# Weight pages moved to 96 bytes past a multiple of 128, and every product's passes as 256-column matmuls

## The chip, the cores and the metric

The kernel runs on one core of one Trainium2 chip. The metric is the device time of one execution in microseconds; the kernel before takes 2318.54 us (median of three runs, 2314.81 to 2322.06).

## The reference, cut to what matters

One layer of an encoder on 512 frames of 2048 features, all in float32: an input projection, banded attention and gated linear attention, an output projection, a gated MLP with a short convolution, a gate from a per-layer embedding, and norms between them.

```python
proj = h @ w_in                                   # then attention and GLA
x = x + concat([y_a, y_g]) @ w_out
u = causal_depthwise_conv(h @ w_ffn_up, w_ffn_conv, b_ffn_conv)
u_gate, u_val = split(u, 2)
x = x + (gelu(u_gate) * u_val) @ w_ffn_down
x = x + sigmoid(rms_norm(x) @ w_ple_gate) * (p @ w_ple_proj)
return rms_norm(x)
```

Nearly all the work is in the matrix products with `w_in`, `w_out`, `w_ffn_up`, `w_ffn_down` and `w_ple_gate`.

## The kernel before, in words

**Three passes.** A float32 product is made of three matmul passes on the format float32r. Each weight page is split into a high part (`wh`, made by ScalarE with a Copy) and a low part (`wl`, made by VectorE as raw minus high), and the operand in the same way. The passes are high weights by high operand, high weights by low operand, low weights by high operand. In each matmul the weights are the stationary operand (loaded by a weight load of 128 columns) and the operand x is the moving one.

**Units and products.** From the attention on, work goes in units. A unit is two blocks of 128 output rows by the two 256-column halves of the frames, computed with seven products in place of eight (P1 to P7, from sums of weight blocks L11, L12, L21, L22 and sums of operand halves R11, R21, R22, N1, N2, T3, T4). One product is kb blocks of 128 by three passes: kb is 8, or 7 in two of the three parts of the down projection. The stages are `in` (12 units, beside the attention), `wo` (8), `up` (44), `dn0` to `dn2` (8 each, kb 8, 7, 7) and `pg` (8). `collect` (L515 to L540) adds a product's PSUM bank into the output page `u`: the first product of a quarter is copied by ScalarE, the others added by VectorE, 128x256 at a time.

**Joined products.** In the middle units of the stages `wo`, `up`, `dn` and `pg` (all but the first two and last two: 4, 40, 4 in each of the three, and 4, so 60 units), products P2, P3 and P4 (`JOINED`, L34) are issued otherwise: the first two passes share the weights, so one matmul of 512 columns reads the high and the low half of x (two runs of 256 that lie 4096 bytes apart) and writes both halves of the bank; the third pass adds into the first half (L495 to L505). `collect` then needs a second VectorE addition of 128x256 for the second half (L536, L537).

**Places in SBUF.** Where a tile begins in its partition follows from the order and sizes of the pools. The pool `pages` holds the weight pages and the pages for x-independent data (`r0`.., `h0`.., `l0`.., `u0`, `u1`, `c0`); behind it lies `h` (the input operand's 16 tiles, moving or stationary in the first 317 us), later replaced by `xb` (operand tiles N1, T3, R22, T4), which begins with a small tile `pad`. From the right end, behind a tile `shim`, lie first the tiles of the gated linear attention, and later `xa` (operand tiles R11, R21, N2). Then come `att` (Q, K and so on of the attention) and `late` (more pages for raw weights and outputs). In this program the begins are, as the remainder by 128 bytes:

| tiles | before | after |
|---|---|---|
| `pages`: weight pages, high and low parts | 0 | 96 |
| `h`: the input operand's tiles | 0 | 96 |
| `xa`, `xb`: the operand tiles of all units | 32 | 32 |
| `att` (Q, K), `late` | 32 | 32 |

All blocks inside these tiles are multiples of 512 bytes, so the remainder holds for every matmul of such a tile. Three products at the very end of `pg` take their weights from operand tiles of `xa` (name `last`), so both operands of these begin at 32.

**What sets the order.** From the attention on, VectorE, ScalarE and TensorE keep the program's order; a table (`agenda`) says after which product each step is issued. A raw page that comes free is refilled at once by SyncE's queue or, where a sum of two blocks is wanted, by GpSimd's accumulating DMA.

Of the kernel before, what the change touches and what calls it, by code (L numbers as in the profile page):

```python
# [8 lines left out]
F32 = mybir.dt.float32  # L9
# [3 lines left out]
ALU = mybir.AluOpType  # L13

P = 128
T = 512
# [14 lines left out]
            "PP": ("L11", None, None)}  # L31
PLAIN = ("P1", "P2", "P6", "P5", "P7", "P3", "P4")
HALVES = ("P1", "P2", "P6", "P7", "P4", "P5", "P3")
JOINED = ("P2", "P3", "P4")  # L34
RINGS = {"wr": ("r0", "r1", "r2"), "wh": ("h0", "h1", "h2"), "wl": ("l0", "l1", "l2")}
FRONT_RINGS = {"u": ("u0", "u1"), "c": ("c0",), "x": ("r6",)}
BACK_RINGS = {"u": ("u2", "u3", "u0", "u1"), "c": ("c1", "c2", "c0"), "x": ("x0", "x1")}
# [5 lines left out]
def encoder_block(ctx: ExitStack, tc: tile.TileContext, A, out):  # L43
    nc = tc.nc
# [4 lines left out]
    pg = ctx.enter_context(tc.tile_pool(name="pages", bufs=1))  # L49
# [7 lines left out]
    class InOrder:  # L57
        def __init__(self, engine):
            self.engine, self.on = engine, False
# [11 lines left out]
    vec, act, ten = InOrder(nc.vector), InOrder(nc.scalar), InOrder(nc.tensor)  # L71
# [26 lines left out]
    def page(ring, name, dt=F32, shape=(P, 1024)):  # L98
        tags = rings[ring]
        i = counts.get(ring, 0)  # L100
        counts[ring] = i + 1
        tag = tags[i % len(tags)]
        return page_pool(tag).tile(list(shape), dt, tag=tag, name=name)
# [99 lines left out]
    def slot(i, name, dt=F32R):  # L203
        return hp.tile([P, 2, T], dt, tag=f"h{i}", name=name)

    pairs = [pg.tile([P, 2, T], F32, tag=t, name=f"pair_{t}") for t in PAIR_TAGS]

    def xslot(i, name):
# [54 lines left out]
    xa, xb = [], []  # L263
# [35 lines left out]
    def xtile(op, g, name, dt=F32R):  # L299
        pool = xa[0] if X_TAGS.index((op, g)) < 6 else xb[0]  # L300
        return pool.tile([P, 2, 1024], dt, tag=f"{op}{g}", name=name)
# [10 lines left out]
    class Stage:  # L312
        def __init__(self, name, units, kb, xd, weights, after, sums, edge, last=PLAIN, begin=None, begin_at=0,
                     chained=False, pace=None, late=(), single=False):
            self.name, self.kb, self.xd, self.weights, self.after = name, kb, xd, weights, after
            self.begin, self.begin_at, self.pace, self.late = begin, begin_at, pace, late
            self.chained, self.tail, self.quarter = chained, [None, None], None
            self.n = (4, kb - 4 - 2 * chained)
            self.x = {}
            n = len(units)  # L320
            self.units = [Unit(self, u, last if i >= n - 2 else PLAIN, edge if i < 2 or i >= n - 2 else sums)
                          for i, u in enumerate(units)]
            for i in range(n):
                self.units[i].pos = i
            if single:
                self.groups = [[u] for u in self.units]
                return
            self.units[0].first = True
            for i in range(2):
                self.units[i].head = i  # L330
                self.units[n - 2 + i].last = i
            self.groups = [self.units[:2]] + [[u] for u in self.units[2:-2]] + [self.units[-2:]]
            for u in self.units[2:-2]:
                u.joined = JOINED

        def load(self, op, g):
            w = self.n[g] * 256
# [21 lines left out]
    class Unit:  # L359
        def __init__(self, stage, u, order, sums):  # L360
            self.stage, self.u, self.order, self.sums = stage, u, order, sums
            self.first, self.head, self.last = False, None, None
            self.w, self.tag = {}, {}
            if sums == "dma":
                self.uses = dict(L11=2, L12=2, S1=2, S2=2, S3=1, L22=1)
                self.made = {"S2", "S4"}
            else:
                self.uses = dict(L11=3, L12=2, S1=2, S2=2, L21=2, L22=2)
                self.made = {"S1", "S2", "S3", "S4"}
            self.parts = dict(C11=2, C12=2, C22=2, C21=1)  # L370
            self.have = set()
            self.left = dict(A=4, B=1, C=2)
            self.o = None
            self.banks = {}
            self.joined = ()

    free = [f"r{i}" for i in (3, 4, 5)]
    wanted = []
# [65 lines left out]
    def prep(i, own=None):  # L444
        prep_low(prep_high(i, own))
# [32 lines left out]
    def bank(name):  # L478
        tag = banks.pop(0)
        return tag, pp_.tile([P, T], F32, tag=tag, name=name)  # L480

    def product(unit, prod, at=None, between=None):
        if prod == "PP":
            return embedding(unit)
        _, op, b = PRODUCTS[prod]
        fresh = b not in unit.banks
        if fresh:
            unit.banks[b] = bank("acc" + b)
        both = unit.banks[b][1]
        t = both[:, 0:256]  # L490
        hi, lo = unit.w[prod]
        st = unit.stage
        kb = st.kb
        kw = {} if fresh else {"skip_group_check": True}
        if prod in unit.joined:  # L495

            for p in range(2):
                for k in range(kb):
                    x = st.x[op, k // 4][:, :, k % 4 * 256:k % 4 * 256 + 256]
                    w = (hi, lo)[p][:, k * P:k * P + P]  # L500
                    if p == 0:
                        ten.matmul(both.rearrange("p (h t) -> p h t", h=2), w, x, start=fresh and k == 0, stop=k == kb - 1, **kw)
                    else:
                        ten.matmul(t, w, x[:, 0], start=False, stop=k == kb - 1, skip_group_check=True)
            return  # L505

        for p in range(3):
            for k in range(kb):
                if p * kb + k == at:
                    between()  # L510
                x = st.x[op, k // 4][:, p % 2, k % 4 * 256:k % 4 * 256 + 256]
                w = (hi, hi, lo)[p][:, k * P:k * P + P]
                ten.matmul(t, w, x, start=fresh and p == k == 0, stop=p == 2 and k == kb - 1, **kw)

    def collect(unit, prod):  # L515

        if prod == "PP":
            return
        b = PRODUCTS[prod][2]
        tag, t = unit.banks[b]  # L520
        t = t[:, 0:256]
        unit.left[b] -= 1
        if unit.left[b] == 0:
            banks.append(tag)
        if unit.o is None:
            unit.o = page("u", "u").rearrange("p (s t) -> p s t", s=2)
        quarter, sign = {"P1": ("C11", 1), "P2": ("C11", 1), "P6": ("C12", 1), "P5": ("C22", -1),
                         "P7": ("C22", -1), "P3": ("C12", 1), "P4": ("C21", -1)}[prod]
        s, h = int(quarter[1]) - 1, int(quarter[2]) - 1
        dst = unit.o[:, s, 256 * h:256 * h + 256]  # L530
        if quarter not in unit.have:
            unit.have.add(quarter)
            act.activation(dst, t, AF.Copy, scale=float(sign))
        else:
            vec.tensor_tensor(dst, dst, t, ALU.add if sign > 0 else ALU.subtract)
        if prod in unit.joined:  # L536
            vec.tensor_tensor(dst, dst, unit.banks[b][1][:, 256:T], ALU.add if sign > 0 else ALU.subtract)  # L537
        unit.parts[quarter] -= 1
        if unit.last is not None and unit.stage.quarter and unit.parts[quarter] == 0:
            unit.stage.quarter(unit, quarter)  # L540
# [328 lines left out]
    for a, b in zip(stages[3:], stages[4:]):  # L869
        i0 = base[a.units[-1]]  # L870
        for n, p in enumerate(PLAIN):
            op = PRODUCTS[p][1]
            for g in range(2):
                start = 2 * n + 2 + g
                if g and b.chained:
                    start = max(start, 5)
# [10 lines left out]
    for n, p in enumerate(PLAIN):  # L887
        op = PRODUCTS[p][1]
# [4 lines left out]
        at, k = ((8, 1), (8, 1), (9, 1), (12, 1), (11, 3), (12, 3), (13, 3))[n]  # L893
# [60 lines left out]
    both = slice(0, 2)  # L954
# [78 lines left out]
            (nc.scalar if c else nc.sync).dma_start(vad[4 * c:4 * c + 4, :, t].rearrange("b p v -> p b v"),  # L1033
                              vstage[c, t].rearrange("p (b v) -> p b v", b=4))

    shim = ctx.enter_context(tc.tile_pool(name="shim", bufs=1, side="right")).tile([P, 240], F32, tag="shim", name="shim")
    nc.gpsimd.memset(shim, 0.0)
    with ExitStack() as mix:
        vp = mix.enter_context(tc.tile_pool(name="v", bufs=1, side="right"))

        with ExitStack() as gctx:
# [8 lines left out]
            for i in range(2):  # L1050
                t = gp.tile([P, T], F32, name=f"attnT{i}")
# [25 lines left out]
            for kt in range(KD):  # L1077
                w = glh[:, kt * 32:kt * 32 + P]
# [117 lines left out]
            st = gla_proj(0)  # L1196
            for hd in range(1, 4):
                nxt = gla_proj(hd)
                gla_core(hd - 1, *st)
                st = nxt  # L1200
# [19 lines left out]
    def operands_left():  # L1220
        hctx.close()
        xb.append(ctx.enter_context(tc.tile_pool(name="xb", bufs=1, reuse_waits="tile")))
        pad = xb[0].tile([P, 8], F32, tag="pad", name="pad")
        nc.gpsimd.memset(pad, 0.0)
        for op in ("N1", "T3", "R22", "T4"):
            for g in range(2):
                front.load(op, g)
        free.extend(("r0", "r1", "r2"))
        issue()
        prep(0)  # L1230
        prep(1)
        for g in range(2):
            front.split("N1", g)
# [16 lines left out]
    for i, (unit, prod) in enumerate(steps[:-4]):  # L1250
        st = unit.stage
# [6 lines left out]
        for k, f in todo:  # L1258
            if k == 1:
                f()  # L1260
        prep_low(coming)
        product(unit, prod)
        for k, f in todo:
            if k > 1:
# [5 lines left out]
        if i - len(steps) in EARLY:  # L1270
            p, op, g = EARLY[i - len(steps)]
            t = xtile(op, g, "last")
# [53 lines left out]
    lo, hi = lo_half, hi_half  # L1326
# [105 lines left out]
```

## Time and profile before

| | |
|---|---|
| median of 3 runs | 2318.54 us (2314.81 to 2322.06) |
| span of the profiled execution, first to last instruction | 2315.0 us |
| mean granted TensorE clock | 0.994 |
| TensorE busy | 2269.1 us, 16564 matmuls |
| VectorE busy | 1957.4 us |
| ScalarE busy | 1295.4 us |
| DMA | 223 GB/s on average |

The profiled execution's own time is its span of 2315.0 us and what lies around it; the median lies 3.5 us above the span. PE is TensorE, PEld its weight loads, DVE VectorE, ACT ScalarE, POOL GpSimd, SP SyncE. A row of the timeline merges matmuls of one kind that follow each other: start, time from the first's start to the last's end, then what it is and how many. Since matmuls overlap, the time from one start to the next (the pitch) is what a matmul costs; it is had from the starts of two rows, divided by the count of the first.

### The profile page before, as it was taken

How to read it: one execution, taken by the hardware profiler on the slowest of the kernel's cores; microseconds unless marked ns; L12 is line 12 of the kernel's file. 1: busy time of each engine (PE TensorE's matmuls, PEld its weight loads, DVE VectorE, ACT ScalarE, POOL GpSimd, SP SyncE). 2: the span in 40 equal slices, each digit the busy share in tenths (PEclk: the TensorE clock that was granted, in tenths of full speed). 3: DMA queues.
4: the chain of work that ended last, by engine and by line, in shares of the span. 5: the costliest groups of instructions: out<-in, count | busy, mean ns of one | idle time of the engine just before them, and what ended most of it. 6: DMA issues, size and time to landing. Idle time of an engine off the chain costs nothing.

```text
span 2315.0 us, 42243 instructions
## 1 busy us (share of the span) xinstructions
PE 2269.1 (98%) x16564; PEld 2122.6 (92%) x16564; DVE 1957.4 (85%) x2753; ACT 1295.4 (56%) x1894; POOL 143.1 (6%) x180
## 2 busy tenths in 40 slices
PE   9999999999999999999999999999999999999996
PEld 8878889999989999999999999999999999999995
DVE  7556358888779888999999999999898797999997
ACT  6344356777555565555555555555564554656655
POOL 0000000000000000000000000000000100000100
PEclk9999999999999999999999999999999999999998
DMA  6522486666978977787877777777866967879994
GB/s 221 195 76 88 168 286 168 177 182 185 314 244 269 309 219 201 214 220 213 219 211 214 206 218 207 218 210 217 261 213 222 316 216 250 282 241 331 273 288 160
DMA packets 195464, 516.48 MB, mean 223 GB/s; under 512 B 20896, under 2 KB 72352, under 8 KB 195264
## 3 DMA queue, kind: packets, MB, share of 16 engines
q1 hardware_dynamic: 165184, 421.49, 51.9%
q0 software_dynamic: 23616, 84.95, 20.8%
q10 hardware_dynamic: 6464, 7.34, 0.9%
q8 instruction: 130, 2.13, 0.4%
q14 instruction: 70, 0.57, 0.1%
HBM read 435.05 MB, written 76.55 MB: 221 GB/s over the span
## 4 chain that ended last, share of the span: by engine, by line
PE 86%; DVE 6%; DMA 4%; ACT 2%; issue 2%; ACTq 0%; DVEq 0%; SPq 0%; POOL 0%; POOLq 0%
PE accA L65 39%; PE accC L65 20%; PE accB L65 10%; PE v L250 2%; PE v L251 2%; PE v L252 2%; DVE wl L65 1%; DMA s<-in_w_blk 1%; DVE u L65 1%; PE pp L65 1%; PE py L65 1%; PE ptr L65 1%; DVE s L65 1%; PE psc L65 1%; PE pk L134 1%
## 5 line engine op out<-in xcount | busy, mean ns | idle before, releaser
L65 DVE TENSOR_TENSOR wl<-s,wh 128x1024 fp32r<-128x1024 f32 (+1 forms) x365 | 437.3, 1199 | 47.3 <-ACT wh L65 46.3
L65 ACT ACTIVATE wh<-l 128x1024 fp32r<-128x1024 f32 (+1 forms) x308 | 318.8, 1037 | 174.9 <-PE accC L65 110.2
L65 ACT ACTIVATE wh<-s 128x1024 fp32r<-128x1024 f32 (+1 forms) x365 | 377.6, 1037 | 48.1 <-DVE s L65 31.8
L65 DVE TENSOR_TENSOR wl<-l,wh 128x1024 fp32r<-128x1024 f32 (+1 forms) x308 | 367.8, 1194 | 39.8 <-ACT wh L65 39.5
L65 ACT ACTIVATE u<-accA 128x256 f32<-128x256 f32 x290 | 109.4, 377 | 339.1 <-PE accA L65 338.9
L65 DVE TENSOR_TENSOR s<-s,l 128x1024 f32<-128x1024 f32 (+1 forms) x192 | 229.5, 1195 | 13.9 <-DMA s<-in_w_blk 12.7
L65 PE MATMUL accA<-up_T,wh 128*128 128x256 f32 (+1 forms) x1088 | 178.6, 313 | 0.2 <-ACT u L65 0.2
L65 PEld LDWEIGHTS accA<-up_T,wh 128*128 128x128 f32 x1088 | 150.1, 188 | 11.4 <-ACT u L65 0.4
L65 DVE SCALAR_TENSOR_TENSOR cv<-u,cw,cv 128x511 f32<-128x511 f32 (+1 forms) x176 | 131.5, 747 | 3.1
L408 POOL DMA_DIRECT2D s<-in_w_up x88 | 75.1, 853 | 788.4 <-DVE u L65 256.7
L65 DVE TENSOR_TENSOR u<-u,accC 128x256 f32<-128x256 f32 x158 | 66.1, 418 | 44.2 <-PE accC L65 41.5
L251 PE MATMUL v<-wv_l,h 128*128 128x512 f32 x256 | 100.5, 392 | 0.0
L250 PE MATMUL v<-wv_h,h 128*128 128x512 f32 x256 | 100.3, 392 | 0.0
L252 PE MATMUL v<-wv_h,h 128*128 128x512 f32 x256 | 99.9, 391 | 0.0
L65 PE MATMUL accA<-up_T,wl 128*128 128x256 f32 x704 | 96.3, 279 | 0.0
L65 ACT ACTIVATE cv<-u,cw 128x512 f32<-128x512 f32 x88 | 67.1, 810 | 51.9 <-DVE u L65 51.9
L65 PEld LDWEIGHTS accA<-up_T,wl 128*128 128x128 f32 x704 | 91.2, 188 | 3.7
L65 PE MATMUL accA<-dn_T,wh 128*128 128x256 f32 (+1 forms) x616 | 90.4, 296 | 2.8 <-ACT wh L65 2.8
L65 PE MATMUL accB<-up_R,wh 128*128 128x512 f32 (+1 forms) x384 | 91.2, 380 | 1.9 <-DVE up_R L65 1.3
L65 PE MATMUL accA<-up_R,wh 128*128 128x256 f32 x704 | 89.7, 279 | 0.0
L65 PE MATMUL accA<-up_N,wh 128*128 128x256 f32 x704 | 89.3, 279 | 0.1
L65 PE MATMUL accC<-up_N,wh 128*128 128x256 f32 x704 | 89.2, 279 | 0.0
(386 smaller groups left out, 5123.2 us busy)
## 6 DMA issues: line engine op xcount, KB each, us to landing
l<-in_w_up SPq DMA_DIRECT2D x132, 512.0 KB, 5.1
s<-in_w_up SPq DMA_DIRECT2D x88, 512.0 KB, 4.6
s<-in_w_up POOLq DMA_DIRECT2D x88, 512.0 KB, 5.7
l<-in_w_dn SPq DMA_DIRECT2D x56, 448.0 KB, 5.0
l<-in_w_blk SPq DMA_DIRECT2D x36, 512.0 KB, 5.1
l<-in_w_out SPq DMA_DIRECT2D x28, 512.0 KB, 5.2
l<-in_w_dn SPq DMA_DIRECT2D x28, 512.0 KB, 5.3
s<-in_w_blk SPq DMA_DIRECT2D x24, 512.0 KB, 4.5
```

Of the source, the lines that this page charges most:

```text
L65: ins = f(*args, **kw)
L134: nc.tensor.matmul(po, whi, act[:, 1, :], start=False, stop=False)
L250: nc.tensor.matmul(ps[t], h1[kt][:, 0, sl], wh, start=kt == 0, stop=False)
L251: nc.tensor.matmul(ps[t], h1[kt][:, 0, sl], wl, start=False, stop=False)
L252: nc.tensor.matmul(ps[t], h1[kt][:, 1, sl], wh, start=False, stop=kt == KD - 1)
L408: nc.gpsimd.dma_start(t, src("L22" if name == "S1" else "L11"), accum_op=ALU.add)
```

## The change

Two things are done. A tile `lead` of 24 floats is put ahead of the pages, so `pages` and `h` begin 96 bytes later; `shim` and `pad` are resized so that `xa`, `xb`, `att` and `late` keep their remainder by 128 (the tiles themselves lie 128 bytes further on). And no product is joined any more: the branch in `product`, the second addition in `collect` and the marks on units go.

```diff
-JOINED = ("P2", "P3", "P4")
...
+    lead = pg.tile([P, 24], F32, tag="lead", name="lead")
+    nc.gpsimd.memset(lead, 0.0)
     pairs = [pg.tile([P, 2, T], F32, tag=t, name=f"pair_{t}") for t in PAIR_TAGS]
...
-            for u in self.units[2:-2]:
-                u.joined = JOINED
...
-        if prod in unit.joined:
-
-            for p in range(2):
-                for k in range(kb):
-                    x = st.x[op, k // 4][:, :, k % 4 * 256:k % 4 * 256 + 256]
-                    w = (hi, lo)[p][:, k * P:k * P + P]
-                    if p == 0:
-                        ten.matmul(both.rearrange("p (h t) -> p h t", h=2), w, x, start=fresh and k == 0, stop=k == kb - 1, **kw)
-                    else:
-                        ten.matmul(t, w, x[:, 0], start=False, stop=k == kb - 1, skip_group_check=True)
-            return
-
...
-        if prod in unit.joined:
-            vec.tensor_tensor(dst, dst, unit.banks[b][1][:, 256:T], ALU.add if sign > 0 else ALU.subtract)
...
-    shim = ctx.enter_context(tc.tile_pool(name="shim", bufs=1, side="right")).tile([P, 240], F32, tag="shim", name="shim")
+    shim = ctx.enter_context(tc.tile_pool(name="shim", bufs=1, side="right")).tile([P, 208], F32, tag="shim", name="shim")
...
-        pad = xb[0].tile([P, 8], F32, tag="pad", name="pad")
+        pad = xb[0].tile([P, 16], F32, tag="pad", name="pad")
```

On TensorE, the product P2 of a middle unit of `up` (bank `accB`, operand tiles `up_R`, weights `wh` and `wl`) stands in the program before as

```order
L65 MATMUL accB<-up_R_8319,wh 128x512 x4
L65 MATMUL accB<-up_R_8362,wh 128x512 x4
L65 MATMUL accB<-up_R_8319,wl 128x256 x4
L65 MATMUL accB<-up_R_8362,wl 128x256 x4
L65 MATMUL accA<-up_N_8396,wh 128x256 x4
```

and in the changed program as

```order
L64 MATMUL accB<-up_R_8405,wh 128x256 x4
L64 MATMUL accB<-up_R_8448,wh 128x256 x4
L64 MATMUL accB<-up_R_8405,wh 128x256 x4
L64 MATMUL accB<-up_R_8448,wh 128x256 x4
L64 MATMUL accB<-up_R_8405,wl 128x256 x4
L64 MATMUL accB<-up_R_8448,wl 128x256 x4
L64 MATMUL accA<-up_N_8482,wh 128x256 x4
```

Eight matmuls of 512 columns have become sixteen of 256; the rest stands where it stood. On VectorE, the rows from the scaling of one unit's output (`u<-u,rb`) to the next unit's product P3 (bank `accC`) are before

```order
L65 TENSOR_TENSOR u<-u,rb 128x1024
L65 TENSOR_TENSOR wl<-s_13111,wh 128x1024
L65 SCALAR_TENSOR_TENSOR cv<-u,cw,cv 128x511
L65 SCALAR_TENSOR_TENSOR cv<-u,cw,cv 128x510
L65 TENSOR_TENSOR wl<-s_12850,wh 128x1024
L65 TENSOR_TENSOR u<-u,accB 128x256 x2
L65 TENSOR_TENSOR s_13111<-s_13111,l_12806 128x1024
...
L65 TENSOR_TENSOR wl<-l_12997,wh 128x1024
L65 TENSOR_TENSOR u<-u,accC 128x256 x2
```

and in the changed program

```order
L64 TENSOR_TENSOR u<-u,rb 128x1024
L64 TENSOR_TENSOR wl<-s_13568,wh 128x1024
L64 SCALAR_TENSOR_TENSOR cv<-u,cw,cv 128x511
L64 SCALAR_TENSOR_TENSOR cv<-u,cw,cv 128x510
L64 TENSOR_TENSOR wl<-s_13279,wh 128x1024
L64 TENSOR_TENSOR u<-u,accB 128x256
L64 TENSOR_TENSOR s_13568<-s_13568,l_13235 128x1024
...
L64 TENSOR_TENSOR wl<-l_13447,wh 128x1024
L64 TENSOR_TENSOR u<-u,accC 128x256
```

The doubled additions have become single ones; nothing else has changed places. ScalarE's order is the same throughout.

More of the change, by code (lines that the diff above doesn't have):

```diff
@@ L374, in __init__ @@
             self.banks = {}
-            self.joined = ()
     free = [f"r{i}" for i in (3, 4, 5)]
@@ L488, in product @@
             unit.banks[b] = bank("acc" + b)
-        both = unit.banks[b][1]
-        t = both[:, 0:256]
+        t = unit.banks[b][1][:, 0:256]
         hi, lo = unit.w[prod]
```

## The prediction

> **What bounds the kernel now.** I read the page's busy times first, then the busy times by stretch, then the timeline of TensorE.
>
> ```profile
> PE 2269.1 (98%) x16564; PEld 2122.6 (92%) x16564; DVE 1957.4 (85%) x2753; ACT 1295.4 (56%) x1894; POOL 143.1 (6%) x180
> PE 86%; DVE 6%; DMA 4%; ACT 2%; issue 2%; ACTq 0%; DVEq 0%; SPq 0%; POOL 0%; POOLq 0%
> ```
>
> ```profile
> core 0: us, PE busy (x) PEld busy (x) DVE busy (x) ACT busy (x) POOL busy (x), PEclk, DMA share, GB/s
> 583.00:690.00 107.00, 99.59 (x786) 95.26 (x785) 79.89 (x104) 61.96 (x90) 6.81 (x8) 1.00 0.89 285
> 850.00:1800.00 950.00, 946.24 (x7043) 896.29 (x7043) 873.84 (x1097) 506.69 (x680) 74.22 (x87) 1.00 0.76 216
> 2170.00:2315.00 145.00, 122.78 (x917) 116.18 (x916) 123.52 (x156) 81.34 (x120) 8.51 (x10) 0.92 0.73 230
> ```
>
> TensorE is busy 2269 of 2315 us and carries 86% of the chain that ended last. The 46 us in which it is idle lie mostly at two places: 7.4 us at the change from `in` to `wo` (first stretch) and 22 us at the end (last stretch). In the long middle it is busy 946 of 950 us at the full granted clock. So the time is the number of matmuls times their pitch, and the question is what the change does to the pitch. VectorE is second, 874 of 950 us in the middle; DMA has room (a share of 0.76).
>
> The pitch is read from starts. Two products of a middle unit of `up`, the first plain, the second joined:
>
> ```profile
> 1199.78 2.03 PE L65 MATMUL accC<-up_N,wh 128*128 128x256 f32 x16
> 1201.65 1.09 PE L65 MATMUL accC<-up_N,wl 128*128 128x256 f32 x8
> 1202.58 0.63 PE L65 MATMUL accA<-up_T,wh 128*128 128x256 f32 x4
> ```
>
> ```profile
> 1205.38 2.03 PE L65 MATMUL accC<-up_R,wh 128*128 128x512 f32 x8
> 1207.25 1.09 PE L65 MATMUL accC<-up_R,wl 128*128 128x256 f32 x8
> 1208.18 2.03 PE L65 MATMUL accA<-up_T,wh 128*128 128x512 f32 x8
> ```
>
> The plain product takes 1202.58 - 1199.78 = 2.80 us for 24 matmuls, 116.7 ns each. The joined one also takes 2.80 us (1208.18 - 1205.38): its 512-column matmuls cost 1.87 / 8 = 233.5 ns, exactly two plain ones. **So joining gains TensorE nothing as things lie now**, and undoing it by itself costs TensorE nothing. I call 256 columns a slot, joined or not. There are 80 units with kb 8 (12 `in`, 8 `wo`, 44 `up`, 8 `dn0`, 8 `pg`) of 7 x 3 x 8 = 168 slots and 16 with kb 7 of 147: 15,792 slots, 1,843 us of the 2,315.
>
> **What a begin can do to the pitch.** The kernel holds three other pairings. In the first stage both operands begin at a multiple of 128 (512 columns); in the scores of the attention both at 32 past (512 columns); in the three last products of `pg` (weights `last`) both at 32 past, with 256 columns as in a unit:
>
> ```profile
> 59.69 0.39 PE L250 MATMUL v<-wv_h,h 128*128 128x512 f32 x1
> ...
> 61.96 0.39 PE L251 MATMUL v<-wv_l,h 128*128 128x512 f32 x1
> ```
>
> ```profile
> 395.43 0.40 PE L65 MATMUL psc<-Kh,Q 128*128 128x512 f32 x1
> 395.66 0.40 PE L65 MATMUL psc<-Kl,Q 128*128 128x512 f32 x1
> 395.90 0.39 PE L65 MATMUL psc<-Kh,Q 128*128 128x512 f32 x1
> 396.13 0.39 PE L65 MATMUL psc<-Kl,Q 128*128 128x512 f32 x1
> 396.36 0.52 PE L65 MATMUL accA<-in_T,wh 128*128 128x256 f32 x3
> ```
>
> ```profile
> 2288.80 3.28 PE L65 MATMUL accC<-pg_R,last 128*128 128x256 f32 x26
> 2291.92 0.38 PE L65 MATMUL ms<-acc,ones 128*128 128x256 f32 x1
> ```
>
> Ten pitches from 59.69 to 61.96 give 227.0 ns, or 113.5 per slot. The scores take 0.93 / 4 = 232.5 ns. The last products take 3.12 / 26 = 120.0 ns. So a slot costs 113.5, 116.7 or 120.0 ns, in steps of 3.3 ns, with nothing different but the begins (and the columns). The weight load of the next matmul runs beside the current one:
>
> ```profile
> L65 PEld LDWEIGHTS accC<-up_N,wh 128*128 128x128 f32 x704 | 85.2, 188 | 0.0
> L65 PEld LDWEIGHTS accC<-pg_R,last x48: 187/192/338, 2283.5 to 2291.7; 128*128 128x128 f32 x48
> ```
>
> A load is recorded with 188 ns, longer than the pitch of a slot, and with 192 where the pitch is 120. So in a 256-column stream a load is under way all the time, and the slower the stream, the longer the load: the two reads get in each other's way. My theory is that what counts is the **distance between the begins of weights and moving operand**: at distance 0 (`last`) a slot costs 120.0 ns, at 32 bytes (all units) 116.7; at 64, where the change puts them (96 against 32), one more such step gives 113.3, the slot of the first stage. That this is a floor is my reading: no fp32r row of 256 or 512 columns shows less per slot.
>
> **The change part by part.** (1) 15,720 slots (all but the 72 of `last`, whose begins stay together) go from 116.7 to 113.3 ns: 15,720 x 3.33 = -52.4 us. Where TensorE waits for others, a faster pitch is not all kept: the two stretches above have 786 + 917 = 1703 matmuls, and if half of what they save is lost in waits, that is 1703 x 3.33 / 2 = +2.8 us. (2) The first stage: 768 matmuls for the values (256 in each of three lines) and 384 for the keys and queries of the linear attention now have both operands at 96. Bounds: 0, since the distance stays 0, and +6.6 us, if two operands off a multiple of 128 cost what the scores cost, 1152 x (232.5 - 227.0) = 6.3 us. A gain has no row: 113.5 is the least seen. I take +6.3, since the scores are the nearest row. (3) 180 second additions go from VectorE:
>
> ```profile
> L65 DVE TENSOR_TENSOR u<-u,accC 128x256 f32<-128x256 f32 x158 | 66.1, 418 | 44.2 <-PE accC L65 41.5
> PE accA L65 <- DVE wl L65: 4.6, 5, 1.3
> PE accC L65 <- DVE u L65: 2.5, 1, 2.5
> ```
>
> 180 x 0.418 = 75 us of VectorE's 1957. TensorE hides nearly all of it already: the rows of its waits for `wl` and `u` show 7 us. I count -2 us. It matters as cover, though: in the middle stretch VectorE's 874 us lose 120 x 0.418 = 50 and become 824, against 950 x 113.3 / 116.7 = 923 us of TensorE, so VectorE stays behind it and does not become the bound. (4) ScalarE and VectorE read and write pages at 96 in place of 0. The pages of `last` lie at 32 and cost the same as a page at 0:
>
> ```profile
> L65 ACT ACTIVATE last<-s x3: 1044/1045/1051, 2260.8 to 2274.3; 128x1024 fp32r<-128x1024 f32 x3
> L65 ACT ACTIVATE wh<-l 128x1024 fp32r<-128x1024 f32 x252 | 266.0, 1057 | 154.1 <-PE accC L65 97.1 <-PE accA L65 33.7 <-PE v L252 8.8
> L65 DVE TENSOR_TENSOR last<-s,last x3: 1216/1225/1227, 2263.5 to 2275.4; 128x1024 fp32r<-128x1024 f32 x3
> L65 DVE TENSOR_TENSOR wl<-l,wh 128x1024 fp32r<-128x1024 f32 x252 | 307.1, 1219 | 34.2 <-ACT wh L65 33.8 <-ACT sc L65 0.3
> ```
>
> 1045 against 1057 and 1225 against 1219: 0. The same bytes are moved by DMA; 5.1 us to landing within a unit of 19.6 us is cover enough:
>
> ```profile
> l<-in_w_up SPq DMA_DIRECT2D x132, 512.0 KB, 5.1
> ```
>
> Sum: -52.4 + 2.8 + 6.3 - 2 = -45.3 us on the span of 2315.0, so 2269.7; the median lies 3.5 above the span: **2273 us**.
>
> **The rivals.** *First, the begin itself costs, and distance is nothing (slower).* An operand that does not begin at a multiple of 128 costs 3.3 ns a slot, weights and moving operand alike. This gives 113.5 with both at 0, 116.7 with one at 32, 120.0 with both at 32: all three rows, and the joined ones too, where the distance theory has to say that in a 512-column matmul the load covers only a part, and does not explain why those cost 233.5 and not 227. For the distance theory speaks only that a load and a stream of the same rate collide steadily when they start alike. With 96 like 32, every slot goes to 120.0: +52.4 us; the first stage +6.3; VectorE -2. 2318.5 + 56.7 = 2375 us. It decides from the first unit on: any pitch above 116.7 in `up` is its sign.
>
> *Second, neither counts at this place (no change).* 32 and 96 could be alike as distances to the other operand. The pitch stays 116.7, and what is left is the first stage, 0 to +6.3, and VectorE, -2: 2316 to 2323 us. The Trainium skill (TensorE: Matmul & The Clock Gate, "Step-by-step: what each phase is for") has TensorE read the two operands through two independent ports, by which the begins should not matter at all; by that rule the 120.0 of `last` would not be there, and the trace disagrees.
>
> *Third, the step is larger or smaller.* A slot of 115 ns would give 15,720 x 1.67 = 26 us less than now, so about 2297. Below 113.3 there is no row. The same page ("Back-to-back issue gap") gives 256 / 2.4 + 2.5 = 109.2 ns for an isolated 256-column matmul; by that figure, an estimate, the sum would be 15,720 x 7.5 = 118 us and the time near 2208, and no row here comes near it.
>
> *That the change doesn't do what it says* is out: the program's tiles begin at 96, and 1416 matmuls of 512 columns have become 2832 of 256.
>
> **How the numbers follow.** Forecast (113.3 ns) 0.48, own range 2255 to 2290; third rival, a step of another size but down, 0.10; second 0.08; first 0.34. I put the forecast above the first rival because the load's own record lengthens with the pitch, which is a collision of two reads and not a price of one, and because a collision is settled by where two streams stand to each other; the first rival fits the rows with fewer words, so it keeps a third. The range runs from 2250 (forecast less the first stage's loss and some more) to 2380 (first rival and 5 us). A measurement of this kernel tells about 0.3%, 7 us, from no change. Faster by more than that: 0.48 + 0.10 = 0.58, less 0.01 for ends near it: 0.57. Within: 0.08. Slower: 0.34 + 0.01 = 0.35.
>
> **What would show it.** In the timeline of `up`: a plain product in 2.72 us (113.3) proves step 1, 2.88 us (120.0) the first rival, 2.80 the second. Ten pitches in the first stage: 2.27 us as now, or 2.33. TensorE busy should be 98% or more in the middle still; if VectorE is above 95% there with TensorE waiting for `wl`, the cover of step 3 was too thin. The split's rows at 1057 and 1219 ns should stand. The prediction is wrong if any of the 256-column pitches rises.

## The result, and the profile after

The changed kernel takes **2326.7 us** (median; 2319.6 to 2333.3) against 2318.8 us (2314.8 to 2324.2) for the kernel before on the same chip: a ratio of 1.0033, 95% interval 1.0023 to 1.0042. The forecast was 2273 us. The profiled execution has a span of 2323.4 us, 8.4 more than before. Its busy times:

```profile
PE 2279.0 (98%) x17980; PEld 2197.7 (95%) x17980; DVE 1892.1 (81%) x2573; ACT 1295.5 (56%) x1894; POOL 143.5 (6%) x181
```

TensorE is busy 9.9 us longer (2269.1 before) and idle as long as before (44.4 us, 45.9 before). So the loss lies in the pitch, not in waits. The middle stretch, busy time and count by engine:

```profile
850.00:1800.00 950.00, 947.07 (x8032) 945.24 (x8032) 822.00 (x964) 503.98 (x677) 73.57 (x86) 1.00 0.76 215
```

VectorE has 822 us of work there, 52 less than before, as forecast, and the granted clock is 1.00 as before. The timeline of TensorE in `up`, three plain products in a row and the start of the next:

```profile
1201.03 2.05 PE L64 MATMUL accC<-up_N,wh 128*128 128x256 f32 x16
1202.91 1.10 PE L64 MATMUL accC<-up_N,wl 128*128 128x256 f32 x8
1203.85 2.05 PE L64 MATMUL accA<-up_T,wh 128*128 128x256 f32 x16
...
1209.51 0.75 PE L64 MATMUL accA<-up_T,wh 128*128 128x256 f32 x5
```

1209.51 - 1201.03 = 8.48 us for 72 matmuls: 117.8 ns, where before had 116.7 and the forecast 113.3. But another stretch of the same trace, same stage, same begins, reads otherwise:

```profile
862.58 1.98 PE L64 MATMUL accA<-up_N,wh 128*128 128x256 f32 x16
...
884.34 1.98 PE L64 MATMUL accC<-up_N,wh 128*128 128x256 f32 x16
886.15 1.07 PE L64 MATMUL accC<-up_N,wl 128*128 128x256 f32 x8
887.15 2.16 PE L64 MATMUL accA<-up_T,wh 128*128 128x256 f32 x16
889.15 1.10 PE L64 MATMUL accA<-up_T,wl 128*128 128x256 f32 x8
```

884.34 - 862.58 = 21.76 us for eight products, 192 matmuls: **113.3 ns, the forecast to the digit**. At 887.15 the stream starts 0.09 us late (886.15 + 8 x 0.1133 = 887.06), the matmul behind it by about as much again (the row takes 2.16 us, where such a row takes 2.05 in the slow stretch above), and from there on the stream stands at 117.8 to the end of `up`. So the two pitches occur with nothing different but what came just ahead. Sorting the 256-column matmuls of the units by the mean pitch of their run, 632 stand at 113.3 and some 15,000 at 117.8. The slower one is no noise: the starts of nine matmuls in a row span 1060 ns (117.78 each) to within 1 ns, in 6,982 matmuls without a break, and the faster one has three in 340 ns.

The first stage kept its pitch, with both operands now at 96:

```profile
59.74 0.39 PE L252 MATMUL v<-wv_l,h 128*128 128x512 f32 x1
...
62.01 0.39 PE L253 MATMUL v<-wv_h,h 128*128 128x512 f32 x1
```

Ten pitches in 2.27 us, 227.0 ns as before. The additions and the split of the weight pages:

```profile
L64 DVE TENSOR_TENSOR u<-u,accC 128x256 f32<-128x256 f32 x98 | 41.1, 419 | 58.3 <-PE accC L64 57.0
```

```profile
L64 ACT ACTIVATE wh<-l 128x1024 fp32r<-128x1024 f32 x252 | 266.0, 1057 | 160.8 <-PE accC L64 94.5 <-PE accA L64 35.0 <-PE v L253 8.8
```

60 additions and 25.0 us less on this bank (66.1 before), 75 us over the three banks; the split at 1057 ns, unchanged. VectorE's busy time as a whole falls by 65.3 us (1957.4 to 1892.1): it counts the time in which two records overlap once, so it fell by less than the sum of the additions.

### The profile page after: what moved, and what is told of

Its sections match the earlier page's. It is cut to its first block, busy times and chain, and to the rows that moved or that the text cites. A ratio compares the mean times of both kernels' runs of the same rounds, so it can differ in the third digit from the quotient of the medians.

```text
span 2323.4 us, 44879 instructions
## 1 busy us (share of the span) xinstructions
PE 2279.0 (98%) x17980; PEld 2197.7 (95%) x17980; DVE 1892.1 (81%) x2573; ACT 1295.5 (56%) x1894; POOL 143.5 (6%) x181
## 4 chain that ended last, share of the span: by engine, by line
PE 84%; DVE 7%; DMA 4%; ACT 3%; issue 2%; ACTq 0%; DVEq 0%; POOL 0%; POOLq 0%; SPq 0%
PE accA L64 39%; PE accC L64 20%; PE accB L64 10%; PE v L251 2%; PE v L252 2%; PE v L253 2%; DVE wl L64 2%; DMA s<-in_w_ple_gate 1%; DMA s<-in_w_blk 1%; DVE s L64 1%; PE py L64 1%; PE ptr L64 1%; PE psc L64 1%; DVE u L64 1%; ACT wh L64 1%
## 5 line engine op out<-in xcount | busy, mean ns | idle before, releaser
L64 PE MATMUL accA<-up_T,wh 128*128 128x256 f32 x1408 | 180.3, 280 | 0.0
L64 PEld LDWEIGHTS accA<-up_T,wh 128*128 128x128 f32 x1408 | 171.8, 188 | 0.2
L64 PE MATMUL accB<-up_R,wh 128*128 128x256 f32 x704 | 91.0, 280 | 1.9 <-DVE up_R L64 1.3
L64 PE MATMUL accA<-dn_T,wh 128*128 128x256 f32 x704 | 91.0, 280 | 1.9 <-ACT wh L64 1.9
L64 ACT ACTIVATE u<-accC 128x256 f32<-128x256 f32 x94 | 36.0, 383 | 97.2 <-PE accC L64 97.0
L64 PE MATMUL accC<-up_R,wh 128*128 128x256 f32 x704 | 90.0, 279 | 0.0
```

What stands on the lines that cost most here:

```text
L64: ins = f(*args, **kw)
```

## The experiments

The changed kernel has two edits, and each was first made alone.

**Joining removed alone** (begins as before).

```diff
...
-            for u in self.units[2:-2]:
-                u.joined = JOINED
...
```

> The kernel before with the joining removed alone; every begin as before (weights at 0, operand tiles at 32). Theory A, the pair of begins sets the pitch: 256-column products of up at 116.7 ns per matmul (2.80 us per product) as the plain ones had it, VectorE 75 us less busy, and the time 0 to 3 us under before (2315 to 2319 us). Theory B, the matmuls of 512 columns that came between set the pitch of those behind them: without them the products fall to the 2.83 us (117.9 ns) of the changed kernel, and the time is 5 to 15 us over before (2324 to 2334 us), all of the change's loss. The theory on record (the distance between begins) and its first rival both have nothing change on TensorE: 2316 to 2319 us.

Measured: 2323.6 us (2314.5 to 2327.0 in 12 executions) against 2317.2, ratio 1.0024, interval 1.0013 to 1.0036. Slower, though the prediction had said that joining gains TensorE nothing. But the profiled execution was the fastest of the twelve, 2314.5 us, and does not show what the others lost. Hence a second profile of the same kernel.

> The kernel before with the joining removed alone, a second profile. The first one was of its fastest execution (2314.5 us; up at 116.7 ns throughout); most executions took 2322 to 2327. Theory of two states: an execution of the usual length has a long stretch of up or of the stages behind at 117.5 to 118.5 ns, 5 to 10 us in all; a fast one has none. Rival, waits: the pitches are as in the first profile and TensorE is idle some 8 us longer.

This one took 2329.6 us. The same 600 us of `up` in both, the one of 2314.5 us first (the number behind TensorE's busy time is its count of matmuls):

```profile
1050.00:1650.00 600.00, 600.00 (x5145) 600.00 (x5144) 516.21 (x611) 317.27 (x430) 52.05 (x61) 1.00 0.78 212
```

```profile
1050.00:1650.00 600.00, 600.00 (x5096) 600.00 (x5096) 514.24 (x608) 312.43 (x423) 52.08 (x61) 1.00 0.77 208
```

TensorE never stops in either, and makes 5145 or 5096 matmuls: 116.6 or 117.7 ns. By single starts three take 350 ns in the one and nine 1060 ns in the other, each over 6,982 matmuls. So the old begins have two pitches as well, one program falls into either, and both of these executions kept theirs through nearly the whole of `up`. In the kernel before, 165 of the 180 runs of joined matmuls have a stream at about 116.7 ns behind them, 18 of these with a slower one ahead. In 14 of the others a joined run ended the faster pitch; but no slower stream stayed slow behind one. The first profile alone would have spoken for theory A, and the median speaks for B: joining does not pay by its own pitch, but by what it leaves behind.

**Begins moved alone** (joining kept).

```diff
+    lead = pg.tile([P, 24], F32, tag="lead", name="lead")
+    nc.gpsimd.memset(lead, 0.0)
...
-    shim = ctx.enter_context(tc.tile_pool(name="shim", bufs=1, side="right")).tile([P, 240], F32, tag="shim", name="shim")
+    shim = ctx.enter_context(tc.tile_pool(name="shim", bufs=1, side="right")).tile([P, 208], F32, tag="shim", name="shim")
...
-        pad = xb[0].tile([P, 8], F32, tag="pad", name="pad")
+        pad = xb[0].tile([P, 16], F32, tag="pad", name="pad")
```

> The kernel before with the begins moved as in the change (weight pages and operand h at 96), the joining kept. Theory A: 12,888 matmuls of 256 columns in units cost 117.9 instead of 116.7 ns (+15 us where all of before stands at 116.7, about half of that as the changed kernel shows it), and the 1416 of 512 columns about 229.5 instead of 233.5 ns (the value that matmuls with one operand at 96 and the other at 32 have in the first stage), -5.7 us: 0 to 10 us over before, and a joined product of up takes 2.78 us or less, a plain one 2.83 us. Theory B: the matmuls of 512 columns hold the others at 116.7 or less, products at 2.80 us or under, and the time is 3 to 6 us under before. The theory on record had 113.3 ns here, near 2275 us with the joined ones at 227.

Measured: 2306.8 us (2306.4 to 2309.2), ratio 0.9957, interval 0.9944 to 0.9971: faster than both kernels, by more than theory A allowed and by more than B. So the two edits do not add: alone they give +0.24% and -0.43%, together +0.33%. The timeline of `up` shows why:

```profile
1200.65 2.00 PE L65 MATMUL accC<-up_R,wh 128*128 128x512 f32 x8
1202.48 1.07 PE L65 MATMUL accC<-up_R,wl 128*128 128x256 f32 x8
1203.39 1.99 PE L65 MATMUL accA<-up_T,wh 128*128 128x512 f32 x8
1205.22 1.11 PE L65 MATMUL accA<-up_T,wl 128*128 128x256 f32 x8
1206.16 2.05 PE L65 MATMUL accA<-up_R,wh 128*128 128x256 f32 x16
1208.05 1.10 PE L65 MATMUL accA<-up_R,wl 128*128 128x256 f32 x8
1208.99 2.00 PE L65 MATMUL accB<-up_R,wh 128*128 128x512 f32 x8
1210.82 1.07 PE L65 MATMUL accB<-up_R,wl 128*128 128x256 f32 x8
1211.73 1.98 PE L65 MATMUL accA<-up_N,wh 128*128 128x256 f32 x16
1213.54 1.07 PE L65 MATMUL accA<-up_N,wl 128*128 128x256 f32 x8
1214.45 1.98 PE L65 MATMUL accC<-up_N,wh 128*128 128x256 f32 x16
```

Behind the first joined run, eight matmuls take 0.91 us (1202.48 to 1203.39: 113 ns); behind the second 0.94 (118 ns), and the plain product that follows takes 2.83 us (1206.16 to 1208.99); behind the third 0.91 again, and the plain product 2.72 (1211.73 to 1214.45: 113.3 ns). Each of these three joined runs turns the state over (of the 180 in this kernel, 162 do), and it then stays until the next one. In all, 4,375 of some 12,900 plain matmuls stand at 113.3 ns here. The single pitches of the joined ones follow a cycle of three, and where the cycle stops decides. The first two of these runs, in ns, and what stands behind them:

```
from 1200.65: 229 232 225 230 231 226 229 232, then 113 114 113 ... (113.3)
from 1203.39: 225 230 231 226 229 232 226 229, then 120 117 118 ... (117.8)
```

**The pairs of begins by themselves.** Ahead of the kernel before, 48 matmuls of 256 columns and 24 of 512 for each of the 16 pairs, nothing beside them:

```diff
...
+                for k in range(48):
+                    st = bw[:, 8 * w + k % 8 * P:8 * w + k % 8 * P + P]
+                    mv = bx[:, 8 * x + k % 4 * 256:8 * x + k % 4 * 256 + 256]
+                    nc.tensor.matmul(z[:, :256], st, mv, start=k == 0, stop=k == 47)
...
```

> The kernel before with a stretch added in front whose results nothing uses, some 0.5 ms: for each of the 16 pairs of begins 0, 32, 64, 96 of weights and moving operand, 48 matmuls of 256 columns and 24 of 512 (two runs of 256), in one order and then in the reverse one. Nothing else runs beside it. Distance (on record): 120.0 ns where the begins are equal, 116.7 at 32 or 96 apart, 113.3 at 64 apart. Begin itself (first rival): 113.5 with both at 0, 116.7 with one at 0, 120.0 with none. Theory A: 116.7 at (weights 0, operand 32), 117.9 at (96, 32), 120.0 at (32, 32), the same in both orders. Theory B: the same pair differs between the two orders.

The pair of the change, weights at 96 and operand at 32, in the first order and then in the reverse one:

```profile
158.10 5.26 PE L68 MATMUL mp_wdxb<-bx,bw 128*128 128x256 f32 x45
163.20 0.28 PE L68 MATMUL mp_wdxc<-bx,bw 128*128 128x256 f32 x1
...
215.37 5.69 PE L68 MATMUL mq_wdxb<-bx,bw 128*128 128x256 f32 x47
220.91 0.28 PE L68 MATMUL mq_wdxa<-bx,bw 128*128 128x256 f32 x1
```

5.10 / 45 = 113.3 ns and 5.54 / 47 = 117.9 ns: the same 256 columns at the same begins, by the order alone. Once settled, the four pairs 64 bytes apart have 113.3 or 117.8 ns and nothing else (113.3 at 96/32, 32/96 and 64/0), and the other twelve from 116.7 to 120.0, none of them 113.3; equal begins have 118.7, and 96/96 also 120.0. So the pair matters, as the prediction had it, and a begin that is no multiple of 128 is no cost by itself: both at 0 (118.7) is slower than 96/32. But the prediction's ladder (120.0 with equal begins, 116.7 at 32 apart, 113.3 at 64) does not hold. Weights that begin 32 bytes further on than the operand (32/0, 64/32, 96/64) stand at 120.0, slower than most of the equal begins; and 0/32, the pair of the kernel before, stands at 117.3 in the first order and at 118.7 in the reverse one, where the kernel has 116.7 and 117.8.

**What tips the stream.**

```diff
...
+            for n in list(range(1, 10)) * 2:
+                joins(n)
+                plain(24)
...
```

> The kernel before with a stretch in front whose results nothing uses, some 0.6 ms: for the four pairs of begins 64 apart (weights and operand at 96/32, 32/96, 64/0, 0/64) runs of 24 matmuls of 256 columns, each behind something that disturbs the stream: eight waits for ScalarE, then 1 to 9 matmuls of 512 columns (twice), 1 to 8 matmuls of 256 columns with both begins at 32, 1 to 6 of 128 columns. Theory of two states: every run settles within five matmuls at 113.3 or at 117.9 ns and stays there, which of them depends on what stood ahead, and behind n matmuls of 512 columns it is 113.3 only where the last of them took 231 to 232 ns (from 113.3: n a multiple of 3; from 117.9: n = 2, 5, 8). Rival, the pair alone decides: each of the four pairs has one pitch in all of its runs.

Weights at 96, operand at 32: 1 to 5 matmuls of 512 columns, and 24 plain ones behind each:

```profile
34.22 0.40 PE L72 MATMUL mp_wdxb<-bx,bw 128*128 128x512 f32 x1
34.46 2.99 PE L65 MATMUL mp_wdxb<-bx,bw 128*128 128x256 f32 x24
37.29 0.62 PE L72 MATMUL mp_wdxb<-bx,bw 128*128 128x512 f32 x2
37.75 2.88 PE L65 MATMUL mp_wdxb<-bx,bw 128*128 128x256 f32 x24
40.47 0.85 PE L72 MATMUL mp_wdxb<-bx,bw 128*128 128x512 f32 x3
41.16 2.88 PE L65 MATMUL mp_wdxb<-bx,bw 128*128 128x256 f32 x24
43.88 1.07 PE L72 MATMUL mp_wdxb<-bx,bw 128*128 128x512 f32 x4
44.79 2.99 PE L65 MATMUL mp_wdxb<-bx,bw 128*128 128x256 f32 x24
47.61 1.31 PE L72 MATMUL mp_wdxb<-bx,bw 128*128 128x512 f32 x5
48.76 2.88 PE L65 MATMUL mp_wdxb<-bx,bw 128*128 128x256 f32 x24
51.48 1.53 PE L72 MATMUL mp_wdxb<-bx,bw 128*128 128x512 f32 x6
```

From the start of each 24 to the start of what follows: 2.83, 2.72, 2.72, 2.82, 2.72 us. From 117.8, one matmul of 512 columns leaves the stream there and two bring it to 113.3; three keep it at 113.3, four lose it, and five bring it back: the rule as expected, and the pair 64/0 gives the same list. The pairs 32/96 and 0/64 have both states too, behind other counts. Behind the other disturbances of this run (waits for ScalarE, matmuls with both begins at 32, matmuls of 128 columns), too, the last twelve of every 24 stand at 113.3 or at 117.8 ns. The theory of two states stands, and the pair alone does not decide.

**One joined product in the changed kernel.**

```diff
...
+            if name == "up":
+                self.units[4].joined = ("P2",)
...
```

> The changed kernel with a single joined product, P2 of the fifth unit of up (8 matmuls of 512 columns); all else as changed. Theory of two states: those eight tip the stream from 117.9 to 113.3 ns, and it stays there for the 39 units of up behind (6,552 matmuls), 29.7 us less where no wait tips it back: 2297 us, and 2310 if it is lost half-way. Rival, a joined product only helps itself and its neighbours: at most 168 x 4.5 ns = 0.8 us, 2326 us.

Measured: 2326.5 us median, but the 12 executions fall into two groups: 2293.3 and 2297.4, and ten from 2324.9 to 2330.4. Two reached the time expected; in most the seed did not take. The profiled execution is of the second group:

```profile
899.99 2.00 PE L64 MATMUL accB<-up_R,wh 128*128 128x512 f32 x8
901.84 1.10 PE L64 MATMUL accB<-up_R,wl 128*128 128x256 f32 x8
902.78 2.05 PE L64 MATMUL accA<-up_N,wh 128*128 128x256 f32 x16
```

The eight take 1.85 us (1.83 in the fast turns above), and 0.94 follow: still slow. Their single pitches are 233 236 229 232 226 229 232 226. The cycle began at another place and stopped on 226. So a slow stream has phases of its own, and where the joined run falls in them counts.

**Begins exchanged** (weights at 32, operand tiles at 96, nothing joined).

```diff
-    lead = pg.tile([P, 24], F32, tag="lead", name="lead")
+    lead = pg.tile([P, 8], F32, tag="lead", name="lead")
...
-    shim = ctx.enter_context(tc.tile_pool(name="shim", bufs=1, side="right")).tile([P, 208], F32, tag="shim", name="shim")
+    shim = ctx.enter_context(tc.tile_pool(name="shim", bufs=1, side="right")).tile([P, 224], F32, tag="shim", name="shim")
```

> The changed kernel with the begins exchanged: weight pages and operand h at 32, operand tiles of the units and the attention's at 96, nothing joined. The distance is 64 as in the change. If the two pairs act alike, most of the stream stands at 117.9 ns and the time is that of the change, 2320 to 2333 us. If the operand behind the weights falls into the 113.3 state by itself, as both of its runs in the first stretch of matmuls did, 15,720 x 4.5 ns = 71 us less, near 2260 us.

Measured: 2327.7 us (2324.9 to 2331.5), the change's time, and `up` at 117.8 ns throughout. The exchange brings nothing by itself.

**Steering, first try.** Only three kb steps are joined, in every second middle unit:

```diff
...
+            j = range(unit.joined[prod], unit.joined[prod] + 3)
...
+                    if p == 0 and k in j:
+                        ten.matmul(both.rearrange("p (h t) -> p h t", h=2), w, x, start=fresh and k == 0, stop=False, skip_group_check=True)
+                    elif p != 1 or k not in j:
+                        ten.matmul(t, w, x[:, p % 2], start=fresh and p == k == 0, stop=p == 2 and k == kb - 1, skip_group_check=True)
...
```

> The begins of the change; in every second middle unit of each stage the first two passes of P2, P3 and P4 are joined for three of the kb steps only (three matmuls of 512 columns in a row, at steps 3, 2, 0 where kb is 8 and 0, 2, 3 where it is 7). Theory of two states: matmuls of 512 columns follow a cycle of three (226, 229, 232 ns) and the stream behind is at 113.3 ns only if the last was the third; from 113.3 the cycle starts at its first, so three in a row keep the state; from 117.8 (a cycle of nine matmuls in 1060 ns) the start depends on how many matmuls stand between, and the three places are chosen so that one of them ends on the third within two units. So up is at 113.3 from its second or third joined unit on: 38 units x 168 x 4.44 = -28 us, the other stages -5 to -15 us more: 2280 to 2295 us. Rival, the state is lost at small waits all the time: 2305 to 2325. Rival, only long runs of joined matmuls hold the pitch: 2320 or more.

> As the kernel with three, but four steps joined at each place in place of three. Theory of two states: from 113.3 ns the fourth is the first of a new cycle and tips the stream to 117.8; from 117.8 the usual starts (second of the cycle) end on the second, so it stays there. Up is at 117.8 nearly throughout: 2315 to 2330 us, 25 us or more behind the kernel with three. Rival, joined matmuls help by their number: as fast as with three or faster.

Measured: with three 2322.2 us (2295.9 to 2331.3), ratio 0.9996, interval 0.9971 to 1.0021; with four 2320.0 (2314.7 to 2327.0), 1.0009, 0.9997 to 1.0021. The three missed: only 2 of 12 executions reached 2296 to 2300. The four came out at the time expected, but not 25 us behind the three, and only half by the mechanism: all 26 runs that met a stream at 113.3 ns ended it, but of the 63 that met a slower one 27 brought it to 113.3, so that about a quarter of its `up` stands there and not nearly none. The profiled execution with three shows a trap that I had not seen in my choice of places. In `up`, its three triples come round for ever as

```
P2: 234 235 230   then 89 matmuls at 117.8
P3: 229 232 225   then 16
P4: 233 236 229   then 213, and P2 again as above
```

None stops on 231 or 232. With these rows the rule can be written down. Of 660 runs of joined matmuls at 96/32 and 64/0 in seven profiles (with the two kernels below), all 387 whose last pitch was 231 or 232 have 113.3 ns behind them, and none of the others. From 113.3 the cycle starts at 226 (or 225) in all 350 cases. From 117.8, count the matmuls since the last joined one, and one more if that took 229 or 230: the remainder by three gave the start (0: 229 232 226; 1: 233 236 229; 2: 235 231 232) in all but a handful of some 250 cases without a wait in between. Remainders here are 0, 1 and 1 (89 + 1, 16, 213 + 1).

**Steering, with the rule.**

```diff
-JOINED = {8: dict(P2=3, P3=2, P4=0), 7: dict(P2=0, P3=2, P4=3)}
+JOINED = {8: dict(P2=2, P3=1, P4=0), 7: dict(P2=2, P3=1, P4=0)}
```

> As the kernel with three joined steps, at other places: steps 2, 1 and 0 of P2, P3 and P4. All profiles so far give a rule (311 of 313 places): count the matmuls since the last joined one, and one more if that one took 229; the remainder by three says whether the next three run 229 232 226, 233 236 229 or 235 231 232, and only the last of these leaves 113.3 ns behind. The places before left 89 and 16 matmuls between (remainders 2 and 1), by which two of the three starts, once met, come round for ever in units with kb 8. Now it is 89 and 17 (77 and 14 where kb is 7), remainders 2 and 2, by which every start reaches 113.3 ns within one unit. So up from its third unit, and the last five units of the stages with eight, stand at 113.3 ns in every execution: about 41 x 168 x 4.44 = -31 us in up and -15 to -20 us in the others, against the change's 2327: 2272 to 2290 us, with a spread under 10 us. Rival, the state is not to be steered (small waits decide): again 2296 to 2330 with most at 2322.

Measured: **2289.1 us** (2287.0 to 2291.3), ratio 0.9869, interval 0.9856 to 0.9882: 1.3% faster than the kernel before, and the spread is narrow, though the time lies at the upper end of what was expected. Nothing differs from the kernel that missed but the steps at which three matmuls are joined. A product in `up`:

```profile
1200.90 1.98 PE L65 MATMUL accA<-up_R,wh 128*128 128x256 f32 x16
1202.71 1.07 PE L65 MATMUL accA<-up_R,wl 128*128 128x256 f32 x8
1203.62 1.98 PE L65 MATMUL accB<-up_R,wh 128*128 128x256 f32 x13
```

2.72 us. 10,900 of some 15,100 plain matmuls stand at 113.3 ns, 10,270 more than in the changed kernel: 10,270 x 4.44 = 45.6 us. TensorE's busy time is 41.7 us less than the changed kernel's (2279.0), its idle time 7.5 more (51.9 against 44.4), so the span is 34.2 us shorter, and the median 37.6:

```profile
PE 2237.3 (98%) x17710; PEld 2144.2 (94%) x17710; DVE 1921.6 (84%) x2663; ACT 1295.0 (57%) x1894; POOL 143.1 (6%) x181
```

Every middle unit in place of every second (the slice `self.units[2:-2:2]` becomes `self.units[2:-2]`):

> The same with joined steps in every middle unit in place of every second. It recovers from a wait one unit earlier, but VectorE gets 90 more additions of 0.42 us, and at 113.3 ns a unit of up leaves it 19.0 us for some 18.2 us of work. If its cover is enough: within 3 us of the kernel with every second unit. If not: waits for wl, each a chance of tipping to 117.8 for a few products, 5 to 15 us more.

Measured: 2293.4 us (2288.1 to 2299.1), ratio 0.9889, interval 0.9871 to 0.9906. The intervals overlap; whether VectorE's 90 further additions cost anything stays open.

Last, the same joined triples at the begins of before (`lead` out, `shim` 240, `pad` 8):

> The kernel with three joined steps at the better places (2289.1 us), but with the begins of before: pages and operand h at 0, operand tiles at 32. It tells whether the 30 us come from the joined threes alone or need the begins. Theory of two states: at 0 and 32 the faster state is 116.7 ns, not 113.3, and threes can only hold that: 2310 to 2320 us, no faster than before by more than 0.3%. Rival, the threes are a better way of issuing at any begins: 2285 to 2300.

Measured: 2318.6 us (2310.7 to 2320.8), ratio 0.9990, interval 0.9978 to 1.0002. The triples alone bring nothing; the 30 us need the begins 64 apart, where a stream can settle at 113.3, and something that brings it there.

## Why the prediction was wrong

**Step 1, 113.3 ns for 15,720 slots, -52.4 us: failed, and with it the forecast.** The step took the pitch as a property of the begins ("at 64 ... one more such step gives 113.3"). The figure is right as one of two states: it stands in the trace of the changed kernel, in the bare matmuls, and in most of the steered kernel. What failed is that all slots would be in it. Without joined matmuls the stream was put into the 117.8 state by a start or a small wait, and from 887 us on nothing brought it out but for 14 matmuls: 632 in all at 113.3. Against 116.7 the 117.8 is +1.1 ns a slot. By these counts TensorE should lose 15,000 x 1.11 - 632 x 3.33 - 2,550 x 1.11 = 11.7 us (an estimate; the 2,550 are those that stand at 117.8 in the kernel before already), and its busy time rose by 9.9.

**"Undoing it by itself costs TensorE nothing": failed.** The arithmetic holds (1.87 / 8 is 233.75 and not 233.5, but by single starts the joined matmuls of `up` take 233.3 ns on average, twice 116.7); it is not the whole of it: joining removed alone costs 0.24%. At 0 and 32, too, a stream can settle at 117.8, and behind each of the 18 joined runs that met a slower stream it stood at 116.7 again. The sentence would have needed a row that shows an unjoined middle stage, and before had none. It did show 117.8 beside 116.7, in the stage `in`, while I had read the pitch from `up` alone. These rows of the kernel before were there to be seen, 8.48 us for 72 matmuls:

```profile
337.42 2.05 PE L65 MATMUL accC<-in_N,wh 128*128 128x256 f32 x16
...
345.90 0.28 PE L65 MATMUL accA<-in_T,wh 128*128 128x256 f32 x1
```

**The clause on waits, +2.8,** had nothing to act on, since the pitch did not fall. In the steered kernel, where it did, 7.5 of 45.6 us went into idle time, so a loss of that kind is real, and larger than the 2.8.

**Step 2, first stage, +6.3: wrong in size, it is 0.** 227.0 ns with both operands at 96. Its lower bound was the right one (the upper one is given as 6.6 and worked out as 6.3). **Step 3:** the additions that went make up 75 us, as worked out, and VectorE's busy time fell by 65.3 (52 in the middle against 50); whether the -2 on the end came can't be seen behind the pitch. **Step 4, 0:** the split's row stands at 1057 ns.

**The rivals.** The first (a begin costs by itself, 120 ns) is refuted: units stand at 113.3 or 117.8 ns, not at 120, and both at 0 is slower than 96/32. The sign given for it, any pitch above 116.7 in `up`, did appear, so that sign could not tell it from a second state. The second (neither counts, 2316 to 2323 us) comes nearest in time, because 117.8 is only 1.1 ns above the old pitch, and not by its mechanism: the pitch did change, upward. Its page's rule, the Trainium skill (TensorE: Matmul & The Clock Gate, "Step-by-step: what each phase is for"), goes on to say that loading the next weights takes no read bandwidth from the running matmul. No run here measures that bandwidth, but where the weights begin against the operand does count: with the joining kept, moving the weight pages (and `h`) alone changes the time by 0.43%.

**Why distance was put above the first rival.** The reason given was that a weight load's record lengthens with the pitch. It does not: in the changed kernel a load takes 188 ns on average where the stream stands at 113.3 (862 to 887 us), and 188 where it stands at 117.8 (900 to 1000 us); in the bare matmuls it is 188 at 120.0, too (96/64). So the first rival was put second for a reason that does not hold; and neither it nor the forecast had a place for a state.

**What stays open:** why the chip has these states (two read streams that lock into step fit the rows, but no run here looks inside), and what decides which one the stream takes behind a wait. Of the 5.6 us that `up` lost (869.6 to 875.2 us in the traces) against the 8.2 that 7,392 x 1.11 ns would give, 1.2 lie in the 264 matmuls at 113.3, and 1.6 in delays of single matmuls (what pitches above 130 ns have over a plain one adds up to 5.9 us in the kernel before, and to 4.3 in the changed one).

## What to carry to other kernels

Where TensorE is busy without a gap, its pitch can have several steady states with the same program: before a pitch read in one stage is carried to another, look for every value of it in the trace, at what precedes each, and over several executions. An instruction that is free by its own cost may be what holds the neighbours in the good state, so two edits that are judged one at a time need not add. And if the executions of one kernel fall into groups (2293 to 2297 and 2325 to 2330 us here), one profile shows one group, and an explanation needs a profile of each.

## What the runs showed of the hardware

- At 256 columns of float32r, a settled stream repeats to within 1 or 2 ns: 113.33 ns (three in 340), 116.67 (three in 350), 117.33 (fifteen in 1760), 117.78 (nine in 1060), about 118.3 (eight in 946, at 0/96), 118.67 (fifteen in 1780), 120.00 (three in 360, or six in 720). Which of them occur goes by the two begins, and which of those is taken by what ran ahead. 113.33 was seen only with the begins 64 bytes apart, and no settled stream of 256 columns was faster.
- A state lasts: 6,982 matmuls, 822 us, without a change. Once, delays of some 0.1 us at each of two matmuls in a row were enough to end the fast one.
- Matmuls of 512 columns in two runs of 256, at 96/32, cost 226, 229 and 232 ns in turn once the cycle runs (229 on average, 233.5 at 0/32), and which of the three comes last decides the pitch of what follows.
